# A step's share of projection work is reckoned together with the value products that the step holds

## The chip, the cores and the metric

The kernel runs on one core of a Trainium2 chip. The metric is the device time of one execution in microseconds (us), of which lower is better. The median of three runs of the kernel before is 3205.68 us (3203.6 to 3206.57).

## The reference

One decoder block on 2048 tokens of width 1024, with 16 meta tokens ahead of them. Two mixers run in parallel on one input projection: a stick-breaking attention with 16 heads of 64, and a convolution module with a depthwise causal filter of 31 taps. In the core of it, cut:

```python
proj = x @ w_in                                   # 1024 -> 9 * 1024
q, k, v, z_a, u_c, g_c, z_c, gate_a, gate_c = split(proj)
z = (q @ k.T) * HEAD_DIM ** -0.5                  # per head, causal
attn = sigmoid(z) * prod over later keys of (1 - sigmoid(z))
o = attn @ v
y_a = (o * silu(z_a)) @ w_attn_out
c = silu(layer_norm(causal_depthwise_conv(u_c * sigmoid(g_c), dw_w) + dw_b))
y_c = (c * silu(z_c)) @ w_conv_out
h = sigmoid(gate_a) * y_a + sigmoid(gate_c) * y_c
return layer_norm(ALPHA * x + h @ w_out)
```

## The kernel before

The sequence is done in two halves of 1024 tokens (`hf` 0 and 1). For each half `phase_a` makes the projections, the attention and the depthwise filter, and `phase_b` the two output projections with their gates. `phase_c` is the last projection and the norm, for both halves. The change lies in `phase_a`.

**Steps.** `phase_a` goes through eight pairs of heads, 0 to 7. A pair is a list of steps, `ticks`: one step for each block of 256 queries (`m`) against each block of 256 keys (`j`), from the diagonal `j == m` down to `j == 0`. The first half has 10 steps in a pair, the second 26. What a step issues on TensorE stands in the order of the loop at the end of `phase_a`, since TensorE is scheduled by hand there (`manual_schedule`); the other engines' order is made by a scheduler. In step `i`:

- `turn(p, i)`: 8 transposes (6 on the diagonal) of the attention weights `f` (L519), copied out of PSUM by ScalarE (L523 to L526).
- `scores(p2, i2)`, two steps ahead: 8 score matmuls (L477), sigmoids on ScalarE (L480, L483), a small memset on GpSimd (L484) and then on VectorE a scan over the keys (L499), which the transposes of step `i + 2` need. Scans follow each other, as each takes its start from the one before.
- projections, drawn from a list of jobs by `fd.fill`. A job is one weight chunk of 128 columns; it yields after each group of three matmuls (L156, L157, L158), which counts as 1536 columns where the chunk of tokens is 512 wide. A chunk of tokens is eight groups, and its result is taken out of PSUM by ScalarE and VectorE. Results go through a tag `mm` of two PSUM banks, so a third chunk waits until the first has been taken out. For the keys that is L372 (ScalarE) and L374 (VectorE).
- in some steps (`due`), the value products (`weigh`, L550, with L558 for the meta tokens) of the two or three steps up to it.

The jobs of pair `p + 1` run in the steps of pair `p`. In the first half they are, in order: keys, values, the first half of the queries, gate and input of the convolution, `z`, and in the last two steps the other queries and a gate. In the second half: the pair's own other queries, then for the next pair values, keys, convolution, queries and `z`. When the convolution's input `u` is there (L432, VectorE), the depthwise filter is 62 VectorE instructions of 128x512 (L443, L446), at low priority between the scans. The other VectorE work between them is small: the copy L496 ahead of each scan, L566 (attention times `z`), L393 (queries), L403 (`z`), L228 (a gate), L139 (weights). GpSimd casts the queries (L395).

**The share.** `quota` is how many columns of jobs a step takes. It was what is left, divided by the steps that are left (line 656):

```python
fd, n = (fa, T - 2 - i) if i < T - 2 else (fb, T - i)
quota = fd.left // n
```

`fa` is for all but the last two steps of a pair, `fb` for these two. Two parts of the quota are drawn at fixed places: 1536 columns between the two parts of the scores of a block with `j == 0`, and 3000 ahead of the value products; the rest is drawn at the end of the step. What was drawn early counts, and a share that is used up draws nothing more.

Of the kernel before, what the change touches and what calls it, by code (L numbers as in the profile page):

```python
# [39 lines left out]
def tile_stickbreak_hybrid(ctx: ExitStack, tc: tile.TileContext, t, out: bass.AP):  # L40
# [211 lines left out]
    def phase_a(hf, xh, xl, gate_items):  # L252
# [8 lines left out]
        ticks = [(m, j) for m in range(4 * hf, 4 * hf + 4) for j in range(m, -1, -1)]  # L261
        T = len(ticks)

        due = [0] * T
        for m in range(4 * hf, 4 * hf + 4):
            i, n = ticks.index((m, m)), m + 1
            parts = -(-n // 3)
            for g in range(parts):
                size = n // parts + (g < n % parts)
                i += size  # L270
                due[i - 1] = size
        last0 = max(i for i, (m, j) in enumerate(ticks) if m < 4 * hf + 2)
        lasthi = max(i for i, (m, j) in enumerate(ticks) if j >= 4 * hf)
        VO = 32
        with tc.tile_pool(name=f"pa{hf}", bufs=1) as pa, tc.manual_schedule(engines={mybir.EngineType.PE}):
# [31 lines left out]
            def turn_v(p):  # L307

                dT = pairs[p]["dT"]
                dv = pa.tile([P, 8, P], F32, tag="dv1", name="dv1", bufs=2 - hf)  # L310
                for e in range(2):
                    tp = bank("aT", 2)
                    for b in range(4):
                        c = VO + (4 * e + b) * P
                        nc.tensor.transpose(tp[:, b * P:(b + 1) * P], dT[:, c:c + P], ident)
                    nc.scalar.copy(dv[:, 4 * e:4 * e + 4, :], tp.rearrange("p (b c) -> p b c", c=P))
                pairs[p]["dv"] = [dv]
                if hf == 0:
                    nc.sync.dma_start(out=dv_d[p], in_=dv)

            def turn_vm(p):

                tp = bank("aT", 2)
                nc.tensor.transpose(tp[0:META, 0:P], pairs[p]["dT"][:, VO - META:VO], ident)
                vm = vms[p % 2]
                for s in range(4):
                    nc.scalar.copy(vm[32 * s:32 * s + META, s, :], tp[0:META, own[s // 2]])
                pairs[p]["vm"] = vm
                nc.sync.dma_start(out=vm_d[p], in_=vm)
# [177 lines left out]
            def turn(p, i):  # L507
                m, j = ticks[i]
                m0 = META if j == 0 else 0
                f = live[p, i]  # L510
                aT = []
                for h in range(2):
                    tp = bank("aT", 2)
                    for blk in range(2):
                        for q in range(2):
                            if j == m and blk > q:
                                continue
                            c = m0 + blk * P
                            nc.tensor.transpose(tp[:, (2 * blk + q) * P:(2 * blk + q + 1) * P],  # L519
                                                f[:, 2 * h + q, c:c + P], ident)  # L520
                    a = pa.tile([P, 512], F32, tag="at", name="at", bufs=6)
                    if j == m:
                        nc.scalar.copy(a[:, 0:256], tp[:, 0:256])  # L523
                        nc.scalar.copy(a[:, 384:512], tp[:, 384:512])
                    else:
                        nc.scalar.copy(a, tp)  # L526
                    aT.append(a)
                return aT

            def turn_meta(fm):  # L530

                tp = bank("aT", 2)
                nc.tensor.transpose(tp[:, 0:P], fm, ident)
                a = pa.tile([P, P], F32, tag="am", name="am", bufs=1)
                nc.scalar.copy(a, tp[:, 0:P])
                return a

            def weigh(p, i, aT, am):


                m, j = ticks[i]
                if j == m:
                    live["o"] = bank("o", 1)[:, 0:256]
                o_ps = live["o"]
                dv = pairs[p]["dv"][0] if j // 4 == hf else pairs[p]["dv0"]
                for blk in range(2):
                    b8 = 2 * (j % 4) + blk
                    c = blk * P if j == m else 0
                    for h in range(2):
                        nc.tensor.matmul(o_ps[own[h], c:256], dv[:, b8, own[h]],  # L550
                                         aT[h][:, blk * 256 + c:blk * 256 + 256],
                                         start=(j == m and blk == 0), stop=False)
                if j > 0:
                    return
                vm = pairs[p]["vm"]
                for q in range(2):
                    for h in range(2):
                        nc.tensor.matmul(o_ps[own[h], q * P:(q + 1) * P], vm[:, 2 * h + q, :], am,  # L558
                                         start=False, stop=(q == 1))
                z = pairs[p]["z"][(m - 4 * hf) // 2]  # L560
                og = pa.tile([P, 256], F32, tag="og", name="og", bufs=2 - hf)
                for q in range(2):
                    b = 2 * (m % 4) + q
                    g0 = (b % 4) * P
                    qs = slice(q * P, (q + 1) * P)
                    nc.vector.scalar_tensor_tensor(og[:, qs], o_ps[:, qs], pairs[p]["vL"][:, b:b + 1], z[:, g0:g0 + P],  # L566
                                                   ALU.add, ALU.mult)
                nc.sync.dma_start(out=og_d[p * P:(p + 1) * P, m * 256:(m + 1) * 256], in_=og)
# [11 lines left out]
            for p in range(NPAIR):  # L580
                a, b, n = [], [], p + 1
# [65 lines left out]
            for p in range(NPAIR):  # L647
                if hf == 1:
                    pairs[p]["dv0"] = pa.tile([P, 8, P], F32, tag="dv0", name="dv0", bufs=1)
                    nc.sync.dma_start(out=pairs[p]["dv0"], in_=dv_d[p])  # L650
                    pairs[p]["vm"] = pa.tile([P, 4, HD], F32, tag="vmt", name="vmt", bufs=1)
                    nc.sync.dma_start(out=pairs[p]["vm"], in_=vm_d[p])
                fa, fb, pend = Feed(body[p]), Feed(rest[p]), []
                for i in range(T):
                    fd, n = (fa, T - 2 - i) if i < T - 2 else (fb, T - i)
                    quota = fd.left // n
                    before = fd.left
                    with tc.high_priority(HIGH):
                        aT, am = turn(p, i), None
                    p2, i2 = (p, i + 2) if i + 2 < T else (p + 1, i + 2 - T)  # L660
                    if p2 < NPAIR:
                        with tc.high_priority(HIGH):
                            sc = scores(p2, i2)
                            next(sc)
                        if ticks[i2][1] == 0:
                            fd.fill(1536, i)
                            with tc.high_priority(HIGH):
                                next(sc)
                    if ticks[i][1] == 0:
                        with tc.high_priority(HIGH):  # L670
                            am = turn_meta(live.pop(("fm", p, i)))
                    pend.append((i, aT, am))
                    if due[i]:
                        fd.fill(3000, i)
                        assert len(pend) == due[i]
                        with tc.high_priority(HIGH):
                            for a in pend:
                                weigh(p, *a)
                        pend.clear()
                    live.pop((p, i - 1), None)  # L680
                    if p + 1 < NPAIR:
                        if i == (4 if hf == 0 else next(x for x in range(lasthi, T) if due[x])):
                            assert "dT" in pairs[p + 1]
                            turn_v(p + 1)
                        elif i == 5 and hf == 0:
                            turn_vm(p + 1)
                    fd.fill(quota - (before - fd.left), i)
                    if n == 1:
                        fd.finish(i)
# [157 lines left out]
    with tc.tile_pool(name="bld", bufs=1) as bp:  # L847
        build(bp, 0, *x0, xbufs=2)
        first_gates(bp, *x0, order0[:NF])
        setup()  # L850
    r0 = phase_a(0, *x0, order0[NF:])
    assert all(g[0] != "zc" for g in r0)
    phase_b(0, alloc_x_next, lambda: gates(0, *x0, r0))
# [27 lines left out]
```

## Time and profile before

| | |
|---|---|
| runs, median of 3 | 3205.68 us |
| profiled execution, its own time | 3206.77 us |
| its span, first to last instruction | 3204.9 us |
| TensorE busy | 3059.2 us, 95% of the span |
| VectorE busy | 2151.2 us, 67% |
| ScalarE busy | 1123.5 us, 35% |
| GpSimd busy | 313.3 us, 10% |
| granted TensorE clock, mean | 0.986 of full speed |

The profile is of one execution. Its span is 1.9 us shorter than its own time, which has what lies before the first and behind the last instruction, and its time is 1.1 us over the median. Steps of `phase_a` run from 183 to 1112 us (first half) and from 1485 to 2745 us (second half). Busy shares are means over stages with different limits, so they don't say which engine ends a wait.

### The profile page before, as it was taken

How to read it: one execution, taken by the hardware profiler on the slowest of the kernel's cores; microseconds unless marked ns; L12 is line 12 of the kernel's file. 1: busy time of each engine (PE TensorE's matmuls, PEld its weight loads, DVE VectorE, ACT ScalarE, POOL GpSimd, SP SyncE). 2: the span in 40 equal slices, each digit the busy share in tenths (PEclk: the TensorE clock that was granted, in tenths of full speed). 3: DMA queues.
4: the chain of work that ended last, by engine and by line, in shares of the span. 5: the costliest groups of instructions: out<-in, count | busy, mean ns of one | idle time of the engine just before them, and what ended most of it. 6: DMA issues, size and time to landing. Idle time of an engine off the chain costs nothing.

```text
span 3204.9 us, 46461 instructions
## 1 busy us (share of the span) xinstructions
PE 3059.2 (95%) x17929; PEld 2561.4 (80%) x17929; DVE 2151.2 (67%) x3019; ACT 1123.5 (35%) x2352; POOL 313.3 (10%) x582
## 2 busy tenths in 40 slices
PE   6999999999999998899999999999999999999998
PEld 6997888888887776688778787878777878787877
DVE  6379678669768278416876868686777774436276
ACT  4333343333333244103444444444444434322010
POOL 0000010100100013110000001010100000113100
PEclk9999999999999999999999999999999999999999
DMA  8343443443343499662121212121212122677753
GB/s 301 122 144 112 144 154 105 146 142 124 125 149 126 144 337 336 244 230 81 63 87 61 91 57 91 57 91 57 91 57 91 57 88 83 222 240 259 252 196 104
DMA packets 250620, 453.34 MB, mean 141 GB/s; under 512 B 17497, under 2 KB 137329, under 8 KB 250400
## 3 DMA queue, kind: packets, MB, share of 16 engines
q1 hardware_dynamic: 248096, 441.86, 40.3%
q0 software_dynamic: 2304, 8.52, 0.9%
q8 instruction: 142, 2.33, 0.3%
q14 instruction: 78, 0.64, 0.1%
HBM read 277.16 MB, written 173.15 MB: 141 GB/s over the span
## 4 chain that ended last, share of the span: by engine, by line
PE 65%; DVE 22%; issue 4%; ACT 2%; DMA 2%; POOL 0%; SPq 0%; POOLq 0%; DVEq 0%; ACTq 0%
PE ps_mm L156 12%; PE ps_mm L157 11%; PE ps_mm L158 11%; DVE acc L446 11%; PE ps_o L550 6%; PE ps_z L477 6%; DVE f L499 5%; PE ps_aT L519 5%; PE ps_mm L768 3%; PE ps_mm L766 3%; PE ps_mm L767 3%; DVE wl L139 1%; ACT at L526 1%; PE ps_o L558 1%; PE ps_z L825 1%
## 5 line engine op out<-in xcount | busy, mean ns | idle before, releaser
L156 PE MATMUL ps_mm<-xh,wh 128*128 128x512 f32 (+3 forms) x2656 | 991.6, 373 | 37.2 <-DVE ka L374 20.1
L157 PE MATMUL ps_mm<-xl,wh 128*128 128x512 f32 (+3 forms) x2656 | 970.6, 365 | 3.4 <-DVE xl L210 3.4
L158 PE MATMUL ps_mm<-xh,wl 128*128 128x512 f32 (+3 forms) x2656 | 971.0, 366 | 1.0 <-DMA wl<-kept_in 1.0
L499 DVE TENSOR_TENSOR_SCAN f<-f,d 128x1028 f32<-128x1028 f32 (+1 forms) x288 | 669.9, 2326 | 345.6 <-POOL f L484 203.7
L446 DVE SCALAR_TENSOR_TENSOR acc<-u,dww,acc 128x512 f32<-128x512 f32 x960 | 700.7, 772 | 4.5
L156 PEld LDWEIGHTS ps_mm<-xh,wh 128*128 128x128 f32 x2656 | 505.4, 190 | 129.1 <-issue 51.1
L158 PEld LDWEIGHTS ps_mm<-xh,wl 128*128 128x128 f32 x2656 | 502.8, 189 | 74.0 <-DMA wl<-kept_in 2.2
L157 PEld LDWEIGHTS ps_mm<-xl,wh 128*128 128x128 f32 x2656 | 504.1, 190 | 58.9 <-DVE xl L210 3.7
L526 ACT COPY at<-ps_aT 128x512 f32<-128x512 f32 x448 | 241.6, 590 | 366.8 <-PE ps_aT L519 366.0
L519 PE MATMUL ps_aT<-ident,f 128*128 128x128 f32 x2176 | 287.8, 274 | 28.5 <-DVE f L499 27.6
L519 PEld LDWEIGHTS ps_aT<-ident,f 128*128 128x128 f32 x2176 | 255.1, 141 | 68.9 <-issue 28.0
L477 PE MATMUL ps_z<-ka,q 128*128 128x256 f32 (+1 forms) x1664 | 272.0, 301 | 8.1 <-ACT f L480 7.9
L550 PE MATMUL ps_o<-at,dv 128*64 128x256 f32 (+1 forms) x2304 | 262.1, 373 | 0.0
L483 ACT ACTIVATE f<-ps_z 128x512 f32<-128x512 f32 x448 | 249.5, 621 | 3.8 <-PE ps_z L477 2.0
L477 PEld LDWEIGHTS ps_z<-ka,q 128*128 128x128 f32 x1664 | 226.4, 194 | 21.0 <-ACT f L480 16.9
L550 PEld LDWEIGHTS ps_o<-at,dv 128*64 128x64 f32 x2304 | 151.1, 136 | 98.4 <-issue 40.7
L768 PE MATMUL ps_mm<-ah,wl 128*128 128x512 f32 x512 | 206.1, 403 | 14.1 <-DVE wl L139 6.6
L766 PE MATMUL ps_mm<-ah,wh 128*128 128x512 f32 x512 | 206.1, 405 | 12.7 <-DMA wh<-kept_w_attn_out 4.7
L767 PE MATMUL ps_mm<-al,wh 128*128 128x512 f32 x512 | 205.5, 401 | 6.8 <-DVE al L754 6.8
L139 DVE TENSOR_TENSOR wl<-raw,wh 128x1024 fp32r<-128x1024 f32 x88 | 108.8, 1236 | 129.6 <-ACT wh L138 129.5
L138 ACT CAST wh<-raw 128x1024 fp32r<-128x1024 f32 x88 | 92.2, 1049 | 288.7 <-PE ps_mm L157 248.1
L484 POOL MEMSET f<- 128x4 f32 x288 | 29.6, 105 | 1586.9 <-ACT f L483 799.8
(149 smaller groups left out, 2783.2 us busy)
## 6 DMA issues: line engine op xcount, KB each, us to landing
wh<-kept_in SPq DMA_DIRECT2D x88, 512.0 KB, 3.5
wl<-kept_in SPq DMA_DIRECT2D x88, 512.0 KB, 4.4
raw<-w_in SPq DMA_DIRECT2D x72, 512.0 KB, 4.8
kept_in<-wh SPq DMA_DIRECT2D x72, 512.0 KB, 2.6
kept_in<-wl SPq DMA_DIRECT2D x72, 512.0 KB, 3.1
wh<-kept_w_attn_out SPq DMA_DIRECT2D x24, 512.0 KB, 4.6
wl<-kept_w_attn_out SPq DMA_DIRECT2D x24, 512.0 KB, 5.2
wh<-kept_w_conv_out SPq DMA_DIRECT2D x24, 512.0 KB, 3.6
```

The costliest lines, as they stand in the source:

```text
L156: nc.tensor.matmul(ps, wh[:, k, :], xhk, start=(k == 0), stop=False)
L157: nc.tensor.matmul(ps, wh[:, k, :], xlk, start=False, stop=False)
L158: nc.tensor.matmul(ps, wl[:, k, :], xhk, start=False, stop=(k == KC - 1))
L446: nc.vector.scalar_tensor_tensor(a, u[:, x + k:x + k + w], dww[:, i, k:k + 1], a, ALU.mult, ALU.add)
L477: nc.tensor.matmul(z[:, z0:z0 + nk], qs[h][s][:, tk], kp[h][:, ks0:ks0 + nk], start=(s == 0), stop=(s == 1))
L499: nc.vector.tensor_tensor_scan(ff, ff, dd, 0.0, ALU.mult, ALU.add)
L519: nc.tensor.transpose(tp[:, (2 * blk + q) * P:(2 * blk + q + 1) * P], f[:, 2 * h + q, c:c + P], ident)
L526: nc.scalar.copy(a, tp)
L550: nc.tensor.matmul(o_ps[own[h], c:256], dv[:, b8, own[h]], aT[h][:, blk * 256 + c:blk * 256 + 256], start=(j == m and blk == 0), stop=False)
L766: nc.tensor.matmul(ps, wh[:, k, :], hi[k], start=(k == 0), stop=False)
L767: nc.tensor.matmul(ps, wh[:, k, :], lo[k], start=False, stop=False)
L768: nc.tensor.matmul(ps, wl[:, k, :], hi[k], start=False, stop=(k == KC - 1))
```

## The change

A step's value products are given a cost in the same columns, 2100 for each block of keys and 1000 more where the meta tokens come along, and the share is what makes projections plus value products equal over the steps that are left:

```diff
+        own_cost = [2100 * due[i] + (1000 if j == 0 else 0) for i, (m, j) in enumerate(ticks)]
...
                     fd, n = (fa, T - 2 - i) if i < T - 2 else (fb, T - i)
-                    quota = fd.left // n
+                    mine = own_cost[i:T - 2] if i < T - 2 else own_cost[i:]
+                    quota = (fd.left + sum(mine)) // n - own_cost[i]
```

All instructions are the same as before; projections move between the steps of a pair. Lines behind the new one are numbered 2 higher than in the profile of before (3 from the share on). In a middle pair of the first half the ten steps held 17, 17, 16, 14, 16, 16, 14, 10, 12 and 12 groups of three matmuls; now they hold 16, 19, 14, 16, 19, 12, 15, 9, 14 and 10. In a middle pair of the second half the steps 0 to 23 held 4 groups each and the last two 8 each; now steps 0 to 13 hold 6, 6, 3, 6, 2, 6, 6, 2, 6, 6, 2, 5, 5 and 2, steps 14 to 23 hold 5, 3, 5, 2, 5, 5, 2, 4, 2 and 0, and the last two 10 and 6.

**TensorE, first half, pair 5, from step 0 to step 1.** Before, where the third chunk of the keys (336 wide) begins in the last group of step 0:

```order
L156 MATMUL ps_mm<-xh,wh 128x352
L157 MATMUL ps_mm<-xl,wh 128x352
L158 MATMUL ps_mm<-xh,wl 128x352
L156 MATMUL ps_mm<-xh,wh 128x336
L157 MATMUL ps_mm<-xl,wh 128x336
L158 MATMUL ps_mm<-xh,wl 128x336
L519 MATMUL ps_aT<-ident,f 128x128 x6
L477 MATMUL ps_z<-ka_6338,q_7250 128x256
L477 MATMUL ps_z<-ka_6338,q_7251 128x256
L477 MATMUL ps_z<-ka_6338,q_7250 128x256
```

The same place in the change, where step 0 ends with the second chunk:

```order
L158 MATMUL ps_mm<-xh,wl 128x352
L521 MATMUL ps_aT<-ident,f 128x128 x6
L479 MATMUL ps_z<-ka_6338,q_7250 128x256
L479 MATMUL ps_z<-ka_6338,q_7251 128x256
L479 MATMUL ps_z<-ka_6338,q_7250 128x256
L479 MATMUL ps_z<-ka_6338,q_7251 128x256
L479 MATMUL ps_z<-ka_6339,q_7252 128x256
L479 MATMUL ps_z<-ka_6339,q_7253 128x256
L479 MATMUL ps_z<-ka_6339,q_7252 128x256
L479 MATMUL ps_z<-ka_6339,q_7253 128x256
L156 MATMUL ps_mm<-xh,wh 128x336
L157 MATMUL ps_mm<-xl,wh 128x336
```

The transposes and scores of step 1 have moved ahead of the first group of the third chunk.

**VectorE, second half, pair 3, from the scan for step 20 on.** Before (a scan is the row `f<-f,d`; `acc<-u` is the filter):

```order
L499 SCALAR_TENSOR_TENSOR f<-f,d_12737 128x1028
L446 SCALAR_TENSOR_TENSOR acc<-u,dww,acc 128x512 x2
L496 COPY d_12737<-f 128x4
L446 SCALAR_TENSOR_TENSOR acc<-u,dww,acc 128x512 x3
L499 SCALAR_TENSOR_TENSOR f<-f,d_12737 128x1028
L446 SCALAR_TENSOR_TENSOR acc<-u,dww,acc 128x512 x2
L496 COPY d_12737<-f 128x4
L446 SCALAR_TENSOR_TENSOR acc<-u,dww,acc 128x512 x2
L393 TENSOR_TENSOR q_18802<-ps_mm,q_18801 64x512
L393 TENSOR_TENSOR q_18804<-ps_mm,q_18803 64x512
L446 SCALAR_TENSOR_TENSOR acc<-u,dww,acc 128x512 x4
L499 SCALAR_TENSOR_TENSOR f<-f,d_12737 128x1028
```

The same stretch in the change:

```order
L501 SCALAR_TENSOR_TENSOR f<-f,d_12737 128x1028
L448 SCALAR_TENSOR_TENSOR acc<-u,dww,acc 128x512 x2
L498 COPY d_12737<-f 128x4
L395 TENSOR_TENSOR q_18722<-ps_mm,q_18721 64x512
L395 TENSOR_TENSOR q_18724<-ps_mm,q_18723 64x512
L448 SCALAR_TENSOR_TENSOR acc<-u,dww,acc 128x512 x6
L501 SCALAR_TENSOR_TENSOR f<-f,d_12737 128x1028
L448 SCALAR_TENSOR_TENSOR acc<-u,dww,acc 128x512
L405 TENSOR_TENSOR za<-ps_mm,sg 128x512
L448 SCALAR_TENSOR_TENSOR acc<-u,dww,acc 128x512
L498 COPY d_12737<-f 128x4
L448 SCALAR_TENSOR_TENSOR acc<-u,dww,acc 128x512 x2
```

The two query instructions, with eight of the filter beside them, stand one scan earlier. The filter as a whole starts two scans earlier: `u` of a pair comes ahead of the scan for step 16 and not behind that for step 17, and the scan for step 2 of the next pair has 2 filter instructions ahead of it where it had 7.

**TensorE, second half, pair 3, the end of step 23.** Before:

```order
L477 MATMUL ps_z<-ka_16586,q_17771 128x272
L477 MATMUL ps_z<-ka_16586,q_17772 128x272
L156 MATMUL ps_mm<-xh,wh 128x512
L157 MATMUL ps_mm<-xl,wh 128x512
L158 MATMUL ps_mm<-xh,wl 128x512
L156 MATMUL ps_mm<-xh,wh 128x512
L157 MATMUL ps_mm<-xl,wh 128x512
L158 MATMUL ps_mm<-xh,wl 128x512
L550 MATMUL ps_o<-at,dv_17566 64x256 x4
L550 MATMUL ps_o<-at,dv_17731 64x256 x8
L315 MATMUL ps_aT<-ident,vT 128x128 x8
L156 MATMUL ps_mm<-xh,wh 128x512
```

In the change:

```order
L479 MATMUL ps_z<-ka_16556,q_17771 128x272
L479 MATMUL ps_z<-ka_16556,q_17772 128x272
L552 MATMUL ps_o<-at,dv_17573 64x256 x4
L552 MATMUL ps_o<-at,dv_17731 64x256 x8
L317 MATMUL ps_aT<-ident,vT 128x128 x8
L521 MATMUL ps_aT<-ident,f 128x128 x8
```

No group of projections is left for this step: scores, value products, transposes of the values and the turn of step 24 follow each other. Between the halves, in `phase_b`, the order on the engines is another too, since its scheduler starts from what `phase_a` left.

## Rows read from the trace of the kernel before

**Rows 1.** The page's first part: busy us (share) xinstructions of each engine.

```profile
PE 3059.2 (95%) x17929; PEld 2561.4 (80%) x17929; DVE 2151.2 (67%) x3019; ACT 1123.5 (35%) x2352; POOL 313.3 (10%) x582
```

**Rows 2.** Waits of TensorE, 183 to 1112 us: us in total, times, longest us.

```profile
PE ps_mm L156 <- DVE ka L374: 20.1, 6, 4.0
```

**Rows 3.** Waits of TensorE, 1484 to 2746 us.

```profile
PE ps_aT L519 <- DVE f L499: 27.6, 19, 3.2
```

**Rows 4.** Timeline, pair 5, step 0: start us, us, engine, line, [idle before <-releaser].

```profile
771.57 2.43 DVE L499 TENSOR_TENSOR_SCAN f<-f,d 128x1092 f32<-128x1092 f32 x1
...
777.33 1.06 DVE L374 TENSOR_TENSOR ka<-ps_mm,ka 64x352 fp32r<-64x352 f32 x2
...
778.54 0.39 PE L156 MATMUL ps_mm<-xh,wh 128*128 128x336 f32 x1 [3.21 <-DVE ka L374]
```

**Rows 5.** Timeline of TensorE, second half, pair 3, steps 0 and 2.

```profile
1960.99 0.82 PE L519 MATMUL ps_aT<-ident,f 128*128 128x128 f32 x6
...
1962.59 0.39 PE L156 MATMUL ps_mm<-xh,wh 128*128 128x512 f32 x1
...
1972.04 1.07 PE L519 MATMUL ps_aT<-ident,f 128*128 128x128 f32 x8 [1.95 <-DVE f L499]
```

**Rows 6.** Windows, pairs 0 and 5: us, busy (x) of PE, PEld, DVE, ACT, POOL, clock.

```profile
183.37:205.52 22.15, 21.49 (x149) 20.31 (x147) 21.73 (x34) 9.37 (x24) 1.38 (x3) 1.00 0.28 102
763.84:791.03 27.19, 23.23 (x148) 21.83 (x147) 26.98 (x41) 10.24 (x26) 1.40 (x2) 0.94 0.31 108
779.63:783.04 3.41, 3.41 (x17) 3.41 (x16) 3.33 (x7) 2.17 (x6) 0.48 (x2) 0.50 0.00 0
```

**Rows 7.** Windows, same columns: pairs 0, 2 and 3 of the second half.

```profile
1484.79:1645.07 160.28, 151.46 (x974) 122.87 (x972) 150.93 (x199) 65.42 (x142) 12.69 (x36) 0.98 0.18 63
...
1802.10:1960.99 158.89, 154.83 (x998) 126.03 (x996) 119.54 (x150) 67.67 (x147) 11.31 (x38) 0.99 0.22 75
1960.99:2118.36 157.37, 153.39 (x997) 124.64 (x996) 119.75 (x150) 67.48 (x147) 13.50 (x38) 1.00 0.22 75
```

**Rows 8.** Windows: pair 3, steps 14 and 15, 16 to 20, 21 and 22.

```profile
2042.06:2053.36 11.30, 11.30 (x73) 9.09 (x72) 5.15 (x7) 4.91 (x11) 0.21 (x2) 1.00 0.26 94
2053.36:2081.46 28.10, 28.10 (x188) 23.04 (x187) 27.69 (x36) 12.75 (x27) 1.48 (x5) 1.00 0.23 80
2081.46:2092.62 11.16, 9.52 (x57) 7.88 (x56) 11.10 (x14) 4.74 (x9) 2.04 (x6) 1.00 0.00 0
```

**Rows 9.** Timeline of VectorE, and one row of GpSimd, pair 3, steps 16 to 21.

```profile
2053.56 0.69 DVE L432 TENSOR_TENSOR u<-ps_mm,u 128x512 f32<-128x512 f32 x1 [0.98 <-PE ps_mm L158]
...
2060.89 1.54 DVE L446 SCALAR_TENSOR_TENSOR acc<-u,dww,acc 128x512 f32<-128x512 f32 x2
...
2075.91 2.29 DVE L499 TENSOR_TENSOR_SCAN f<-f,d 128x1028 f32<-128x1028 f32 x1
2078.12 1.39 DVE L446 SCALAR_TENSOR_TENSOR acc<-u,dww,acc 128x512 f32<-128x512 f32 x2
...
2080.83 1.40 DVE L393 TENSOR_TENSOR q<-ps_mm,q 64x512 fp32r<-64x512 f32 x2
2082.26 3.10 DVE L446 SCALAR_TENSOR_TENSOR acc<-u,dww,acc 128x512 f32<-128x512 f32 x4
...
2082.47 1.02 POOL L395 CAST q<-q 64x512 fp32r<-64x512 f32 x1
```

**Rows 10.** Timeline of TensorE, pair 3, step 22.

```profile
2087.71 1.06 PE L519 MATMUL ps_aT<-ident,f 128*128 128x128 f32 x8 [1.50 <-DVE f L499]
...
2089.57 0.39 PE L156 MATMUL ps_mm<-xh,wh 128*128 128x512 f32 x1
...
2090.27 0.40 PE L156 MATMUL ps_mm<-xh,wh 128*128 128x512 f32 x1
```

**Rows 11.** The page's fifth part: xcount | busy us, mean ns | idle before.

```profile
L446 DVE SCALAR_TENSOR_TENSOR acc<-u,dww,acc 128x512 f32<-128x512 f32 x960 | 700.7, 772 | 4.5
```

**Rows 12.** Window: between the steps of the two halves.

```profile
1111.64:1484.79 373.15, 339.03 (x1451) 268.60 (x1450) 193.94 (x297) 102.04 (x158) 75.50 (x61) 0.95 0.75 259
```

## The prediction

> **What bounds the kernel now.** I read the page first: TensorE is busy for 95% of the span, VectorE for 67% [rows 1]. The change moves TensorE's instructions and takes none away, so it can only win or lose where TensorE waits, or where its clock falls behind a wait. The waits of TensorE in the two stretches of steps come next. In the first half the large one is for L374, which takes the keys out of PSUM: 20.1 us in 6 waits [rows 2], one in each of pairs 1 to 6. In the second half it is for the scan: 27.6 us in 19 waits [rows 3].
>
> The timeline of pair 5 shows the first kind. At the end of step 0 TensorE comes to the third chunk of the keys, whose bank the first chunk still holds. The first chunk's L374 stands in VectorE's queue behind a scan that starts at 771.57, and filter instructions, and runs at 777.33; TensorE goes on at 778.54 after 3.21 us [rows 4]. Then a second loss follows: for 3.41 us the granted clock is 0.50, which is the 1.2 GHz level. Steps 0 and 1 take 27.19 us in pair 5 and 22.15 us in pair 0, which had no such wait and kept its clock at 1.00; TensorE is busy 1.74 us longer with the same work [rows 6]. So such a wait costs 3.2 + 1.7 = 4.9 us.
>
> In the second half I read the steps of pair 3. In steps 14 and 15 VectorE is busy for 5.15 of 11.30 us. From step 16 on the depthwise filter fills it: 27.69 of 28.10 us in steps 16 to 20, 11.10 of 11.16 in steps 21 and 22 [rows 8]. There the scan, which has its turn between the filter's instructions, comes late: TensorE waits 1.50 us in front of step 22 [rows 10] and 1.95 us in front of step 2 of the next pair [rows 5]. This stretch is bound by VectorE; the rest of the step list by TensorE.
>
> **The change, first half.** The third chunk now begins in step 1, behind the transposes and scores of that step. VectorE's order up to this L374 has the same instructions, so it comes when it came. For 6 transposes and 8 scores the start of step 0 of pair 3 gives 1.60 us, from 1960.99 to 1962.59 [rows 5]. The scan at 771.57 is already that of step 2 [rows 4]; that of step 1, which these transposes need, is done, so they don't wait themselves. Of 3.21 us 1.60 are filled, 1.61 stay. Does the clock still fall? The wait of 1.50 us lies in a window with the clock at 1.00 [rows 8, 10]. That of 1.95 us in pair 3 left it at 1.00 over the pair too, while pair 2 shows 0.99 and is 1.5 us longer [rows 7]. 1.61 is nearer to 1.50, so I take it that the clock stays up. Gain per pair: 1.60 + 1.74 = 3.3 us, in six pairs 20 us. If the clock falls as before, it is 6 x 1.6 = 10 us; pair 1, with the longest wait (4.0 us), may give 2 us more, so that the bounds are 10 and 22. The other moves of this half meet no wait of size; the scans have their lead of two long steps.
>
> **The change, second half.** Here the question is whether VectorE keeps up in steps 16 to 23. Let the turn of step 16 be time 0 for TensorE without waits.
>
> - VectorE's start. `u`'s first chunk is complete with 64 groups, now the first group of step 14. Steps 14 and 15 take 11.30 us [rows 8] (one group moves from 15 to 14); a first group ends 1.86 + 0.70 us behind its turn [rows 10]. L432 starts 0.2 us later, as it did behind step 15 [rows 8, 9]: at -11.3 + 2.6 + 0.2 = -8.5.
> - VectorE's work up to the scan for step 21, counted in its order: 28 L446, 6 scans, two L432, two L443, two L393, two L566 and small ones. An L446 takes 0.67 us (four between 2078.12 and 2080.83), but 0.79 where only one half of the filter is under way (2060.89 to 2062.35, two); a scan occupies VectorE for 2.21 us (2075.91 to 2078.12); the pair of L393 takes 1.4 us, and the four L446 beside GpSimd's cast 3.10 instead of 2.7 [rows 9]. That is 19 x 0.67 + 9 x 0.79 + 6 x 2.21 + 1.4 + 1.4 (L432) + 1.2 (L443, estimated below an L446 each) + 0.4 + 1.2 for the small ones = 38.7 us, so the scan ends at 30.2.
> - TensorE is there at 28.10 - 0.7 = 27.4, since steps 16 to 20 hold one group less than before [rows 8]. It waits 2.8 us in front of step 21.
> - Up to the scan for step 23 VectorE has 8 L446, one L403 (0.6) and 2 scans, 10.5 us: done at 40.7. TensorE without waits needs 9.52 us busy in steps 21 and 22 [rows 8], less two groups: 8.1 us, so 35.5. The delay is 5.2 us in all. A clock that falls behind the first of these waits is hidden, since VectorE ends the next.
> - Step 23 has no group left. The second part of its scores then waits for a bank and the turn of step 24 for the copy of the values; neither is in the trace, each between nothing and one group (0.7 us); I take half, 0.7 us together.
> - The filter ends earlier in the next pair, so the wait in front of its step 2 goes: two steps of six groups against four give TensorE 2.8 us more there.
>
> So a pair pays 5.2 + 0.7 where it paid 1.50 + 1.95 and some 0.15: 2.3 us more. Pair 2 also paid 1.5 us in clock, which pair 3 did not [rows 7]; I count two such pairs of the six, and this as gone: +0.8. Four pairs at 2.3 make 9.2, two at 0.8 make 1.6; pair 0, which waits most already and runs with a clock of 0.98 [rows 7], I leave at nothing; pair 7 has no filter behind it. Sum +11 us. If the L446 all take 0.66 us a pair pays 1 us less, if 0.73 (700.7 us over 960, [rows 11]) 1.1 us more; pair 0 may give or take 4 us. Bounds: +1 and +24, the upper with a lost clock in each pair.
>
> On the cast beside the filter the Trainium skill, SBUF — State Buffer, "two separate sides", says that GpSimd and a VectorE instruction with two SBUF inputs lock each other out for a whole instruction. By it VectorE would stand still for the cast's whole 1.02 us, where the four L446 beside it are 0.4 us longer [rows 9]: 7 x 0.6 = 4 us more, and 3201 in place of 3197. The row decides here.
>
> **Between the halves** TensorE is idle for 34 us and its clock is 0.95 [rows 12]; the scheduler's new order there moves some of it. I take nothing, with 6 us either way.
>
> Sum: -20 + 11 = -9 us. The profiled execution took 3206.8 us, 1.1 over the median; so the median goes to 3205.7 - 9 = 3197.
>
> **The rivals.** About 0.2%, 6.4 us, is what a measurement of this kernel can tell from no change.
>
> - Both halves gain, as equal steps would let one expect: the scan waits go with the clock they cost. -20 - 27.6 and some 4 us of clock: 3154. For it: VectorE has idle time in steps 14 and 15, which the earlier filter uses. Against it: the two L393 with eight L446 stand one scan sooner, and steps 22 and 23, which follow, have become short. 0.1.
> - The clock falls in the first half all the same: -10 + 11, no change, 3207. For it: 1.61 us lies between a wait that never lowered the clock and one that sometimes did. 0.2.
> - The loss between the halves eats the gain: -9 + 6 = -3, 3203. 0.1.
> - Slower: VectorE's backlog before the scan for step 23. 36 L446 stand there; each 0.01 us more costs 0.36 us a pair. From 0.74 us in the mean, where I have 0.70, the second half loses what the first gains. The mean of all 960 is 0.73 [rows 11], so the point is near. At 0.76, with the clock falling once in each pair behind step 23: 6 x (2.2 + 1.7) = 23 more, 3220. 0.15.
> - The forecast, 3197, with a range of its own from 3189 to 3203: 0.45, of which 0.36 lies below the bound and 0.09 within.
>
> Faster by over 0.2%: 0.1 + 0.36 and 0.04 of the cases between, 0.50. Within: 0.09 + 0.16 + 0.06, 0.31. Slower: 0.15 and 0.04 of the second and third rival, 0.19. The range reaches to the slower case and half-way to the case of both halves: 3178 to 3215.
>
> **What would show it.** Right: the waits for L374 sum to about 10 us and not 20, no stretch at 0.50 behind step 0, and steps 0 and 1 of pair 5 near 24 us. In the second half TensorE waits for the scan in front of steps 21, 22 and 23 (2.8, 1.0 and 1.5 us) and no longer in front of step 2, and a middle pair takes about 159.7 us against 157.37. Wrong: scan waits below 20 us in the second half in all (the second part of the forecast fails), or steps 0 and 1 of the first half still near 27 us (the first).

## The result, and the profile after

The changed kernel takes 3222.28 us (median of four runs, 3221.66 to 3226.78), the kernel before beside it 3204.70: the ratio is 1.0057, 95% interval 1.0045 to 1.0070. It is slower by 0.57%, where 3197 us (3178 to 3215) was forecast. Line numbers below are 2 higher than in the rows of before (3 from the share on); a kernel with added lines moves them again.

The page of the profile after, first and fifth part, as [rows 1, 11]:

```profile
span 3220.5 us, 46479 instructions
...
PE 3056.0 (95%) x17929; PEld 2559.9 (79%) x17929; DVE 2147.2 (67%) x3019; ACT 1121.4 (35%) x2350; POOL 305.8 (9%) x582
...
L448 DVE SCALAR_TENSOR_TENSOR acc<-u,dww,acc 128x512 f32<-128x512 f32 x960 | 705.0, 776 | 4.6
```

TensorE is busy as long as before; the loss is waiting. The windows of four stretches of the kernel after say where: the first half from the turn of its first step to that of its last, what lies between the halves, the second half likewise, and what lies behind it (us, busy of PE, PEld, DVE, ACT, POOL, clock, DMA share, GB/s):

```profile
183.30:1109.30 926.00, 891.89 (x5550) 780.54 (x5548) 701.51 (x1006) 335.41 (x788) 68.29 (x162) 0.99 0.40 136
1109.30:1479.28 369.98, 335.31 (x1444) 265.95 (x1443) 196.38 (x297) 98.95 (x155) 78.81 (x61) 0.95 0.75 261
1479.28:2756.80 1277.52, 1226.70 (x7918) 1001.25 (x7917) 930.67 (x1164) 535.48 (x1160) 88.74 (x290) 0.99 0.22 73
2756.80:3220.50 463.70, 446.09 (x1956) 363.17 (x1954) 234.94 (x404) 85.10 (x130) 62.02 (x46) 0.99 0.64 216
```

Cut at the same steps, before had 928.3, 373.1 [rows 12], 1260.5 and 459.7. So the first half gains 2.3 and not 20, the stretch between gains 3.2, the second half loses 17.1 and not 11, and the stretch behind the steps loses 4.0.

TensorE's waits in the first half after (us in total, times, longest), as [rows 2]:

```profile
PE ps_mm L156 <- DVE ka L376: 14.6, 6, 2.5
PE ps_mm L156 <- DVE sg L228: 5.2, 1, 5.2
...
PE ps_mm L156 <- ACT u L428: 3.9, 7, 0.6
```

The wait for the keys is 2.43 us in pair 5, from 3.21; forecast was 1.61. And seven waits of 0.55 us for L428, the sigmoid of the filter's gate, are new. The windows of pairs 2 and 5 after, and of a stretch behind the wait of pair 5:

```profile
412.45:527.46 115.01, 110.71 (x711) 97.72 (x710) 89.61 (x130) 42.90 (x103) 9.24 (x22) 1.00 0.40 135
759.70:875.72 116.02, 111.95 (x711) 99.24 (x710) 89.50 (x130) 43.00 (x103) 9.24 (x22) 0.99 0.39 133
...
775.66:779.07 3.41, 3.41 (x14) 3.41 (x14) 3.33 (x6) 0.00 (x0) 0.00 (x0) 0.50 0.00 0
```

In pairs 1 and 2 the clock stays at 1.00 behind a wait of 2.4 us and the pair takes 115.0 to 115.2 us; in pairs 3 to 6 it goes to the 1.2 GHz level for 3.41 us and the pair takes 116.0 to 116.1, as long as before (116.1 to 116.2). Steps 0 and 1 of pair 5 take 26.9 us, where the prediction had about 24 as right and near 27 as wrong.

The waits in the second half after, as [rows 3]:

```profile
PE ps_aT L521 <- DVE f L501: 34.4, 21, 4.2
PE ps_mm L156 <- DMA wh<-kept_in: 4.1, 6, 1.9
PE ps_mm L158 <- DMA wl<-kept_in: 3.9, 6, 1.6
PE ps_o L560 <- ACT am L537: 3.2, 1, 3.2
```

The scan waits grew by 6.8 us; that they would grow was forecast. The 8.0 us for weights in step 1 of pairs 2 to 7 were 1.2 us, all in pair 7; no step of the prediction had them.

Two readings go with this. First, why the keys' L376 comes later than forecast. VectorE and GpSimd after, between pair 4 and pair 5 (turn of step 0 at 759.70):

```profile
751.23 1.27 POOL L397 CAST q<-q 64x512 fp32r<-64x512 f32 x2 [1.73 <-DVE q L395]
751.85 2.67 DVE L448 SCALAR_TENSOR_TENSOR acc<-u,dww,acc 128x512 f32<-128x512 f32 x2
...
752.62 1.35 POOL L489 TENSOR_SCALAR_AFFINE_SELECT f<-f 128x1024 f32<-128x1024 f32 x1
...
768.29 2.43 DVE L501 TENSOR_TENSOR_SCAN f<-f,d 128x1092 f32<-128x1092 f32 x1
...
774.05 1.06 DVE L376 TENSOR_TENSOR ka<-ps_mm,ka 64x352 fp32r<-64x352 f32 x2
...
775.26 0.39 PE L156 MATMUL ps_mm<-xh,wh 128*128 128x336 f32 x1 [2.43 <-DVE ka L376]
```

The same place before (turn of step 0 at 763.84):

```profile
754.04 1.52 POOL L487 TENSOR_SCALAR_AFFINE_SELECT f<-f 128x1024 f32<-128x1024 f32 x1
755.26 0.69 DVE L393 TENSOR_TENSOR q<-ps_mm,q 64x512 fp32r<-64x512 f32 x1
755.62 1.63 POOL L395 CAST q<-q 64x512 fp32r<-64x512 f32 x2
755.99 1.81 DVE L446 SCALAR_TENSOR_TENSOR acc<-u,dww,acc 128x512 f32<-128x512 f32 x2
```

From its filter's start, 37.8 us ahead of that turn in both, VectorE does the same instructions without idle time, 43 of them filter steps up to the scan of step 2. After, two of them stand beside GpSimd's casts and select and take 2.67 us, where two together take 1.39 to 1.41 elsewhere; before, the select ran beside L393, which reads PSUM and kept its 0.69 us, and two filter steps beside the casts took 1.81. That is 2.67 - 1.81 = 0.86 us more, and the scan of step 2 starts 8.59 us behind the turn of step 0 where it started 7.73 behind it [rows 4, 6]: also 0.86.

Second, the weight waits. SyncE's queue and TensorE after, second half, pair 3 (turn of step 0 at 1957.97):

```profile
1961.74 0.32 SPq L450 DMA_DIRECT2D c_d<-acc  x1
...
1962.26 0.32 SPq L570 DMA_DIRECT2D og_d<-og  x1
...
1962.67 0.70 SPq L134 DMA_DIRECT2D wh<-kept_in  x1
...
1967.64 0.47 PE L156 MATMUL ps_mm<-xh,wh 128*128 128x512 f32 x1 [0.57 <-DMA wh<-kept_in]
...
1969.92 0.50 PE L158 MATMUL ps_mm<-xh,wl 128*128 128x512 f32 x1 [1.58 <-DMA wl<-kept_in]
```

The weights of the values are asked for 4.7 us behind the turn, since their loads stand behind the stores of the filter's result and of the attention's output, which wait for VectorE. The queue before, where the turn of step 0 is at 1960.99:

```profile
1965.30 0.32 SPq L568 DMA_DIRECT2D og_d<-og  x1
1965.72 0.38 SPq L134 DMA_DIRECT2D wh<-kept_in  x1
```

There too they stood 4.7 us behind the turn, with the filter's store behind them. But the projection of the queries ahead of them, eight groups, now is over early in step 1, so TensorE comes to the values 9.1 us behind the turn; before it came to them in step 2, 12.7 us behind it.

### The profile page after: what moved, and what is told of

Its sections match the earlier page's. It is cut to its first block, busy times and chain, and to the rows that moved or that the text cites. A ratio compares the mean times of both kernels' runs of the same rounds, so it can differ in the third digit from the quotient of the medians.

```text
span 3220.5 us, 46479 instructions
## 1 busy us (share of the span) xinstructions
PE 3056.0 (95%) x17929; PEld 2559.9 (79%) x17929; DVE 2147.2 (67%) x3019; ACT 1121.4 (35%) x2350; POOL 305.8 (9%) x582
## 4 chain that ended last, share of the span: by engine, by line
PE 54%; DVE 30%; DMA 5%; issue 4%; ACT 1%; SPq 0%; POOL 0%; DVEq 0%; POOLq 0%; ACTq 0%
DVE acc L448 15%; PE ps_mm L156 10%; PE ps_mm L158 10%; PE ps_mm L157 10%; DVE f L501 8%; PE ps_z L479 5%; PE ps_o L552 4%; PE ps_aT L521 4%; PE ps_mm L771 2%; PE ps_mm L769 2%; PE ps_mm L770 2%; DVE wl L139 1%; DMA wl<-kept_in 1%; DMA or<-og_d 1%; DVE q L395 1%
## 5 line engine op out<-in xcount | busy, mean ns | idle before, releaser
L156 PE MATMUL ps_mm<-xh,wh 128*128 128x512 f32 (+3 forms) x2656 | 987.9, 372 | 43.3 <-DVE ka L376 14.6
L521 PEld LDWEIGHTS ps_aT<-ident,f 128*128 128x128 f32 x2176 | 248.4, 141 | 86.8 <-issue 47.9
```

What stands on the lines that cost most here:

```text
L156: nc.tensor.matmul(ps, wh[:, k, :], xhk, start=(k == 0), stop=False)
```

## The experiments

The lengths of the four stretches, cut as above, tell most kernels apart (us, in each profiled execution):

| kernel | first half | between | second half | behind |
|---|---|---|---|---|
| before | 928.3 | 373.1 | 1260.5 | 459.7 |
| changed | 926.0 | 370.0 | 1277.5 | 463.7 |
| new share, first half alone | 926.5 | 371.8 | 1260.2 | 458.8 |
| new share, second half alone | 928.2 | 372.7 | 1276.7 | 462.2 |
| changed, keys by ScalarE | 899.6 | 379.2 | 1277.0 | 461.8 |
| changed, stores by GpSimd | 929.4 | 371.3 | 1264.3 | 467.0 |
| changed, cast by ScalarE | 928.6 | 379.7 | 1279.1 | 459.5 |
| changed, half the taps | 926.0 | 373.5 | 1236.2 | 469.7 |
| before, keys by ScalarE | 891.6 | 376.3 | 1260.2 | 460.3 |
| first half and keys | 900.5 | 379.0 | 1260.4 | 459.6 |
| before, keys and stores | 894.0 | 376.7 | 1263.3 | 462.6 |
| changed, keys and stores | 900.6 | 380.6 | 1262.8 | 465.6 |

**One half at a time.** The first kernel sets the costs to nothing in the second half, the second in the first half:

```diff
+        if hf == 1:
+            own_cost = [0] * T
```

> The new share in the first half alone; the second half is shared out as before. Theory (the two halves add up): the trace of the changed kernel has its first half and the stretch between the halves 2.3 + 3.2 us shorter than before, so this kernel takes 3199 to 3204 us, 0.998 to 1.000 of before, and the waits for the keys' evacuation sum to about 14.6 us in six waits with a clock of 0.50 behind some of them. Rival (the 2.3 us are an accident of that one execution, and the first half really gains the 20 us that were forecast): 3185 us and no stretch at 0.50 behind the waits.

> The new share in the second half alone. Theory (the second half and what follows it carry the whole loss): 17 us in the steps and 4 behind them, so 3222 to 3227 us, 1.005 to 1.007 of before, with scan waits in front of steps 21 and 23 of about 2.7 and 1.0 us a pair and waits for the weights of the values in step 1. Rival (the second half loses the 11 us that were forecast, the rest comes from its start behind a shifted first half): 3216 us, and no weight waits in step 1.

Measured: 3205.65 us, 1.0003 (0.9994 to 1.0012), and 3224.15 us, 1.0059 (1.0044 to 1.0074). The first has the six waits for the keys, 14.6 us, and the clock falls behind five of them; its median is 2 us over the expected range, its span of 3200.8 us inside it. The second carries the whole loss, with weight waits of 7.2 us. The halves add up, and both rivals fall. That the first half and the stretch behind it gain anything, 5.5 us in the profiled execution of the changed kernel, the median of the first kernel does not show.

**The keys out of the way.** ScalarE copies the chunk into a spare tile, and the bank is free without VectorE:

```diff
+                    src = ps
+                    if hf == 0:
+                        src = pa.tile([P, 352], F32, tag="kt", name="kt", bufs=3)
+                        nc.scalar.copy(src[:, 0:n], ps)
...
-                            nc.vector.tensor_tensor(ks[h][oth[h], d0:d0 + l], ps[own[h], p0:p0 + l],
+                            nc.vector.tensor_tensor(ks[h][oth[h], d0:d0 + l], src[own[h], p0:p0 + l],
```

> The changed kernel, with the keys of the first half copied out of PSUM by ScalarE into a spare tile, from which VectorE subtracts later; so the bank no longer waits for VectorE. Theory (the wait for the keys' evacuation and the clock behind it hold the first half up): the 14.6 us of waits go to under 3, no stretch at 0.50 behind step 1, pairs 3 to 6 fall from 116.1 to 112.5 us or so, and the whole is 18 to 22 us faster than the changed kernel: 3201 to 3205 us. Rival (VectorE's queue itself is the bound, the bank only the place where it shows): the scan or another result of VectorE is waited for instead, and the time stays at 3218 to 3222.

Measured: 3205.69 us, 1.0001 (0.9991 to 1.0011), 17 us less than the changed kernel. Its waits of TensorE in the first half, from the top:

```profile
PE ps_mm L156 <- DVE sg L228: 5.2, 1, 5.2
PE ps_z L483 <- ACT f L486: 4.0, 14, 0.5
```

and the window of its pair 5:

```profile
744.40:855.48 111.08, 109.99 (x710) 97.73 (x709) 89.63 (x130) 43.96 (x106) 8.85 (x22) 1.00 0.41 139
```

No wait for the keys is left, the clock stays at 1.00 and a pair takes 111.1 us. Waits are 3.0 us less, 2.43 for the keys and 0.54 for L346, which goes too; TensorE is busy 1.9 us less, of which some 0.7 is not the fall of the clock, since pair 2 of the changed kernel, with its clock at 1.00, is busy 110.71 us. In the half that is 26.4 us, more than expected there. The wait was the limit there, and the rival falls. But the whole is 0.7 us over the expected range: 9.2 us come back between the halves, where the edit changes nothing but the scheduler's order; that part was not followed further.

**The stores out of the way.** The two stores of the second half go to GpSimd's queue:

```diff
-                        nc.sync.dma_start(out=c_d[i * P:(i + 1) * P, hf * HALF:(hf + 1) * HALF], in_=acc)
+                        (nc.gpsimd if hf else nc.sync).dma_start(out=c_d[i * P:(i + 1) * P, hf * HALF:(hf + 1) * HALF], in_=acc)
...
-                nc.sync.dma_start(out=og_d[p * P:(p + 1) * P, m * 256:(m + 1) * 256], in_=og)
+                (nc.gpsimd if hf else nc.sync).dma_start(out=og_d[p * P:(p + 1) * P, m * 256:(m + 1) * 256], in_=og)
```

> The changed kernel, with the stores of the filter's result and of the attention's output in the second half issued by GpSimd, so that the weights' loads of the next pair no longer stand behind them in SyncE's queue. Theory (the weights of the values come late because their loads stand behind two stores that wait for VectorE): the weight waits in step 1, 7.8 us in six pairs, go, with the clock lost behind them in pair 3; 8 to 12 us faster than the changed kernel, 3210 to 3214 us. Rival (the transfers themselves are too slow for the shorter projection of the queries): the waits stay above 5 us, 3220 us or over.

Measured: 3211.64 us, 1.0019 (1.0009 to 1.0029), 10.6 us less than the changed kernel, as expected. SyncE's queue at pair 3 (turn of step 0 at 1962.83):

```profile
1962.79 0.32 SPq L134 DMA_DIRECT2D wh<-kept_in  x1
1963.20 0.38 SPq L134 DMA_DIRECT2D wl<-kept_in  x1
```

The loads start with the turn and not 4.7 us behind it, and no wait for weights is left; the second half is 13.2 us shorter. The waits themselves were 8.0 us. Pair 3, where the clock fell behind the weights, goes from 162.5 to 158.3 us, and pair 7, where it fell too, from 157.2 to 152.7: 4.2 us more in the two than their waits, for the most part clock. The Trainium skill, DMA: Bandwidth & Descriptors, "Anatomy of one DMA — SWDGE (gpsimd) path", says that a wait for a semaphore is done by the issuing sequencer, ahead of dispatch. The two start times agree with a queue that stands while its store waits.

**The cast.** To see whether GpSimd makes the keys late, ScalarE does the queries' second cast in the first half:

```diff
-                        nc.gpsimd.tensor_copy(qs[h][1][oth[h]], qs[h][1][own[h]].bitcast(F32))
+                        if hf == 0:
+                            nc.scalar.copy(qs[h][1][oth[h]], qs[h][1][own[h]].bitcast(F32))
+                        else:
+                            nc.gpsimd.tensor_copy(qs[h][1][oth[h]], qs[h][1][own[h]].bitcast(F32))
```

> The changed kernel, with the queries' second cast of the first half done by ScalarE and not by GpSimd. In the trace of the changed kernel the casts and a GpSimd select run beside two filter instructions that take 1.20 and 1.55 us instead of 0.74, and VectorE reaches the scan of step 2 0.86 us later behind the turn of step 0 than before. Theory (that delay is why the wait for the keys is 2.43 us and not 1.6): the six waits sum to about 10 us, the clock stays at 1.00 behind them, pairs 3 to 6 take 114.3 us, and the whole is 6 to 10 us faster than the changed kernel, 3212 to 3216. Rival (the select takes the casts' place beside the same filter instructions): the waits stay above 13 us and the time at 3220 to 3224.

Measured: 3232.53 us, 1.0083 (1.0068 to 1.0098): 10 us slower than the changed kernel. Its waits in the first half:

```profile
PE ps_mm L156 <- DVE ka L376: 12.0, 6, 2.0
PE ps_mm L156 <- DVE q L395: 5.1, 6, 0.8
```

and VectorE and GpSimd ahead of pair 5:

```profile
755.29 3.55 DVE L451 SCALAR_TENSOR_TENSOR acc<-u,dww,acc 128x512 f32<-128x512 f32 x4
...
756.04 1.59 POOL L492 TENSOR_SCALAR_AFFINE_SELECT f<-f 128x1024 f32<-128x1024 f32 x1
```

The wait goes from 2.43 to 1.99 us. Of these four filter steps one takes 1.55 us, the others 0.74 to 0.75 (they overlap at their ends). In the changed kernel the two beside the casts and the select took 1.20 and 1.55; the first is back at 0.74, and 1.20 - 0.74 = 0.46 is what the wait lost, within 0.02. So of the 2.67 - 1.40 = 1.27 us that these two take too long, the casts cost 0.46 and the select, which stays, 0.81. Before, the casts stood beside two filter steps as well, and these took 1.81 - 1.40 = 0.41 us too long. So the casts explain next to nothing of the 0.86 us; nearly all of it is the select's, which no run moves. The six waits, 12.0 us, lie between the theory's 10 and the rival's 13: it was wrong to put the whole delay down to the casts, and right that a GpSimd instruction beside the filter delays the keys. At 1.99 us the clock still fell in all six pairs. The time went otherwise: a new wait of 0.85 us in a pair for the queries, and 9.7 us between the halves, as with the keys.

**The filter's load.** Sixteen of its 31 taps are left out in the second half:

```diff
-                            for k in range(1, TAPS):
+                            for k in range(1, TAPS if hf == 0 else TAPS // 2):
```

> The changed kernel with 15 of the filter's 31 taps in the second half (16 are left out there, so the filter's result is not the reference's): 32 VectorE instructions fewer in each pair, some 22 us. Theory (VectorE's filter backlog causes the scan waits and, through the store behind it in SyncE's queue, the weight waits): scan waits of the second half fall from 34.4 to under 6 us, the weight waits of step 1 to under 2, pairs near 153.5 us; 3178 to 3186 us. Rival (the scans come late for another reason: ScalarE's evacuations or the short steps themselves): scan waits stay above 20 us, 3205 us or over.

Measured: 3189.45 us, 0.9946 (0.9931 to 0.9961), 3 us over the expected range. The second half is 41 us shorter, the stretches around it 10 us longer. Its waits of the second half, from the top:

```profile
PE ps_aT L521 <- DVE f L501: 14.7, 7, 2.3
PE ps_z L479 <- ACT f L482: 2.9, 8, 0.6
```

Waits in front of step 23 and those for weights are gone, so VectorE's load does cause them. One scan wait of some 2.1 us stays in each of pairs 0 to 6, in front of step 21 (20 in pair 0). VectorE ahead of that scan in pair 4:

```profile
2212.79 1.40 DVE L395 TENSOR_TENSOR q<-ps_mm,q 64x512 fp32r<-64x512 f32 x2
2214.22 4.35 DVE L448 SCALAR_TENSOR_TENSOR acc<-u,dww,acc 128x512 f32<-128x512 f32 x5
2218.48 2.29 DVE L501 TENSOR_TENSOR_SCAN f<-f,d 128x1028 f32<-128x1028 f32 x1
```

Five filter steps stand between the queries and the scan even with half the taps; the whole filter has six there. For this wait what stands in the queue ahead of the scan counts, not the length of the filter, and "under 6 us" was wrong for that reason.

**The filter sooner.** The filter's two projections go ahead of the values and keys, in the changed kernel and in that of before:

```diff
-                        a += [job_v(n), job_k(n)] + cv + [job_q(n, 0, last0 - 1), job_z(n)]
+                        a += cv + [job_v(n), job_k(n)] + [job_q(n, 0, last0 - 1), job_z(n)]
```

> The changed kernel, with the filter's two projections put ahead of the values and keys in the list of the second half, so that the filter begins some 32 groups sooner, where VectorE has idle time. Theory (only the place of the backlog costs time): the filter is done before step 20, scan waits under 8 us, no weight waits in step 1, pairs near 154 us: 3178 to 3190 us. Rival (the backlog goes along, and the keys' evacuation and the scans of steps 8 to 16 stand in it): waits as many as now, 3215 to 3225 us.

> The kernel before, with the same exchange in the list of the second half. Theory: the 27.6 us of scan waits go but for a few, and pairs come to 153.5 to 155 us: 3174 to 3184 us. If equal steps are worth something by themselves once VectorE is not behind, the changed kernel with this exchange is faster than this one; if the share is neutral there, both differ by what the first half and the stretches around it differ, under 4 us. Rival as in the other: 3200 us or over.

Measured: 3254.24 us, 1.0152 (1.0135 to 1.0169), and 3260.44 us, 1.0170 (1.0155 to 1.0185). The theory falls. The rival holds in its mechanism, though the changed kernel is 29 us over its 3225. The waits of the changed kernel with this edit, second half:

```profile
PE ps_aT L521 <- DVE f L501: 43.7, 27, 3.2
PE ps_mm L156 <- ACT u L428: 28.4, 1, 28.4
```

Of the waits, 28.4 us are a single one in pair 0, where `u`, of which the second half has one buffer, is still read by that pair's own filter: that was overlooked. In the later pairs the scan waits moved from steps 21 to 23 to steps 13 to 18 and became more; pairs 1 to 6 take 161.0 to 162.4 us, with no wait for weights, against 158.3 to 162.5. With this edit the changed kernel is the faster of the two, by 6.2 us; as VectorE is late in both (scan waits of 43.7 and 41.3 us), that doesn't show equal steps to be worth something by themselves.

**Both waits taken away, under either share.** The keys' copy in the kernel before; in the first half's new share alone; then keys and stores in either kernel (the diffs are those above):

> The kernel before, with the keys of the first half copied out of PSUM by ScalarE into a spare tile. In the changed kernel this took 4.9 us from each of six pairs, 9 came back between the halves. Theory (the wait for the keys and the clock behind it hold up pairs 1 to 6 in either kernel): the 20.1 us of waits go, pairs 2 to 6 fall from 116.15 to 111 us, the first half by 26 to 30, and the whole by 17 to 30 as the stretch between the halves turns out: 3175 to 3188 us. Rival (with the old share another wait of step 0 stands behind this one): pairs stay above 113.5 us, 3190 us or over.

> The new share in the first half alone, with the keys of the first half copied out by ScalarE. Theory (without the wait for the keys the share of the first half is neutral): pairs 1 to 6 take 111.1 us as in the changed kernel with the same copy, the second half 1260 as before; 3175 to 3188 us, within 5 us of the kernel before with the copy. Rival (the new share is worth something by itself in the first half): 5 us or more faster than the kernel before with the copy.

> The kernel before with both changes: keys of the first half copied out by ScalarE, stores of the second half issued by GpSimd. Theory (the old share has only 1.2 us of weight waits to lose): 0 to 3 us below the kernel before with the copy alone, 3173 to 3187 us, scan waits in the second half 26 to 29 us. Rival (the stores on GpSimd hold up its selects in front of the scans): scan waits of 32 us or over, and slower than the copy alone by 4 us or more.

> The changed kernel with both changes, so that neither the wait for the keys nor the weight waits are left in either of this and the kernel before with both. Theory (what the new share then still costs is the scan waits of steps 21 to 23, 31 us against 27.6 and the 1 us of short last steps): its second half is 3 to 8 us longer than that of the kernel before with both, and it takes 3188 to 3197 us, 5 to 15 more. Rival (equal steps are worth something once those waits are gone): faster than the kernel before with both.

Measured, in this order: 3171.68 us, 0.9895 (0.9881 to 0.9908); 3184.28 us, 0.9941 (0.9927 to 0.9954); 3176.80 us, 0.9912 (0.9898 to 0.9925); 3190.74 us, 0.9955 (0.9943 to 0.9968). The first beats both kernels, by 1.05% and 1.6%, and is 3 us below its expected range: its first half falls by 36.7 us and not by 26 to 30. Its waits in the first half, from the top:

```profile
PE ps_mm L156 <- DVE sg L228: 4.4, 1, 4.4
PE ps_z L481 <- ACT f L484: 4.0, 14, 0.5
```

No wait for L428 is there, and pairs 2 to 6 take 110.3 to 110.5 us; with the new share they take 111.1 to 111.2. So in the first half the share is not neutral, as I had expected: without the wait for the keys it costs 8.9 us (0.7 a pair, 1.5 in pair 0, 3.3 in pair 7), in a pair mostly the 0.55 us for L428; the expected "within 5 us" became 12.6. In the second half the expected 3 to 8 us between the last two kernels are not there: 1262.8 against 1263.3 us. That the last one takes 13.9 us more, within the expected 5 to 15, is luck: it comes from the first half (6.6) and the stretches around the second. And against the kernel before with the keys alone, 1260.2, the stores on GpSimd cost the old share 3 us in the second half, 5.1 us in all. The rival of that kernel holds by the time; its waits, 30.6 us, stay just under the 32 that it asked for:

```profile
PE ps_aT L523 <- DVE f L503: 18.4, 15, 3.3
PE ps_aT L523 <- ACT q L395: 12.2, 5, 2.5
```

The wait in front of step 2, the second row, is 2.4 us there and not 1.95. The rows ahead of it in pair 3:

```profile
1939.40 0.54 POOL L452 DMA_DIRECT2D c_d<-acc  x1
...
1939.93 0.19 POOL L488 MEMSET f<- 128x4 f32 x3
1940.09 2.30 DVE L503 TENSOR_TENSOR_SCAN f<-f,d 128x1028 f32<-128x1028 f32 x1 [0.39 <-POOL f L488]
```

GpSimd's small memset, which the scan needs, stands behind the filter's store, and the scan waits 0.39 us for it. So the store holds up this memset, not a select as the rival had it.

## Why the prediction was wrong

- **First half, "1.61 stay"**: failed; 2.43 stayed. What is filled was right: TensorE comes to the third chunk 13.1 us behind the turn, from 11.5. But its ground, that VectorE's order has the same instructions "so it comes when it came", left out that they can become longer beside GpSimd: L376 comes 0.86 us later, some 0.8 of it for the select, which now runs beside a filter step. The kernel with ScalarE's cast shows that GpSimd beside the filter delays the keys; the select's part is read from the trace alone.
- **"I take it that the clock stays up"**: failed in four of six pairs. With 2.43 us the question was another than with 1.61; pairs 1 and 2, where it held, did gain, 3.4 and 1.2 us. The price of a fall was too high: 1.74 us forecast, but with the same wait step 1 takes 15.6 us with a fall and 14.0 without, and the pair 1.0 us more.
- **"The other moves of this half meet no wait of size"**: failed. In the changed kernel the new waits for L428 are 3.9 us in all, pair 7 is 2.1 us longer and pair 0 0.5. Without the wait for the keys such losses are 8.9 us, shown by the two kernels with the keys' copy. Of the 20 us forecast, 2.3 came.
- **Second half, the scan**: right in its places. In pairs 1 to 6 it waits 2.6 to 2.7 us in front of step 21, and then 0.9 and 1.5 in front of steps 22 and 23 or, behind a fall of the clock, 1.0 in front of step 23 alone (2.8, 1.0 and 1.5 were forecast); the wait in front of step 2 is gone. That a fall of the clock behind the first wait is hidden also held: without weight waits (stores by GpSimd) pairs 2 to 6 take 158.1 to 158.3 us with a fall or without. The term was too large: such a pair pays 0.8 us more than pair 3 before [rows 7], not 2.3, and without weight waits the half is 3.8 us longer, not 11. One reading in its sum is off: the two filter steps named for the 0.79 us take 0.73 each, from 2060.89 to 2062.35, and with that the wait in front of step 21 would have been put at 2.3.
- **The middle pair, 159.7 us**: hit (159.4 to 159.9 in four of five) for a partly wrong reason, since 0.7 to 1.1 us of it are waits for weights.
- **Left out**: SyncE's queue. I counted what VectorE does and not which loads stand behind its stores, nor how soon the groups ahead of a load are over. It is worth 10.6 us in the whole and 13.2 in this half, more than the 6 us that the half was off: the scan's term, too large, hid a part of it.
- **Between the halves and behind**: -3.2 and +4.0 us. The first is within the 6 either way that I took; nothing was taken for the second, which ranged from 459 to 470 us in kernels that didn't touch it. What the order does in these two stretches stays open.

Of the rivals, "the clock falls in the first half all the same" is nearest by its mechanism, but ended at 3207. The slower one has nearly the time, 3220, for VectorE's backlog in front of step 23; the runs don't bear that out, since the wait there is 1.0 to 1.5 us.

## What to carry to other kernels

When work is moved between steps, look for each load at two times: when its queue lets it start (what stores stand ahead of it, and whom they wait for) and how soon the work ahead of its use is now over. A wait that the move is to fill is best removed where it is made: freeing the bank with one more ScalarE copy gave 36.7 us in the first half (33 in the whole kernel), where filling the wait with other work gave 2.3. And a queue with the same instructions doesn't take the same time if another engine's work moves beside it.

## What the runs showed of the hardware

- GpSimd beside VectorE's filter steps, which read two SBUF tiles: a cast of 0.60 us made one 0.46 us longer, a select one 0.81 us longer, itself taking 1.59 and not 1.07 us. L393, which reads PSUM, kept its 0.69 us beside a select of 1.52. The Trainium skill, SBUF — State Buffer, "SBUF: two separate sides", has the one that starts first hold a shared pair of ports for its whole instruction. The select's row is nearer to that than the 0.4 us for a cast of 1.02 that the prediction took [rows 9]; the cast's row is not, since there the filter step began 0.04 us ahead of the cast and was the one made longer.
- The granted clock behind a wait of TensorE in the steps, over all fourteen profiles (a stretch at 0.50 that begins between 2.5 us ahead of the wait's end and 2 us behind it): 2 of 91 waits of 1.25 to 1.6 us, 1 of 8 up to 1.8, 21 of 40 up to 2.1, 47 of 77 up to 2.8, and 59 of 67 of 3 us and more. So the same wait has its fall in one pair and not in another. By these counts, 3 of 99 up to 1.8 us, my estimate is that 1.61 us would have kept the clock in most pairs.
